# Turning five of ten groups of attention probabilities by crossbar DMA instead of on TensorE

## The chip, the cores and the metric

The kernel runs on one core of one Trainium2 chip. The metric is the device time of one launch, in microseconds. TensorE (PE) does the matrix products, VectorE (DVE), ScalarE (ACT) and GpSimd (POOL) the rest; SyncE (SP) issues nearly all transfers. All engines run side by side, each through its own instructions in order, and wait for one another by semaphores.

## What is computed

One block of a transformer on 256 rows of 1024 columns, in float32: a mixer whose first half is a pool over windows of 2, 4, 8 and 16 rows and whose second half is self-attention, then cross-attention to 256 rows of memory, then a gated feed-forward with a convolution over three rows.

```python
h = rms_norm(x, norm_mix_g); proj = h @ w_in            # u | q | k | v
q, k = rope(rms_norm(q)), rope(rms_norm(k))             # 8 heads of 64
p = softmax(causal(q @ k.T) / 8)                        # per head, 256 x 256
attn = p @ v
x = x + concat([pool(u) * pool_scale, attn]) @ w_out
h, m = rms_norm(x), rms_norm(mem)
p = softmax(rms_norm(h @ w_xq) @ rms_norm(m @ w_xk).T / 16)   # 4 heads of 256
x = x + (p @ (m @ w_xv)) @ w_xo
up = conv3(rms_norm(x) @ w_up) + conv_b                 # 2 x 2816 columns
x = x + (silu(gate) * val) @ w_down
```

The blocks of the self-attention's mixture are 256 rows long, as the sequence is, so it is plain causal attention here. A softmax is computed with its rows (queries) on partitions; the product with V needs the probabilities with their keys on partitions. So every 128x128 block of them has to be transposed, and these transposes are what the change is about.

## The kernel before

**Weights and precision.** All weights come from one packed tensor in 1 MB chunks (128x2048), loaded by SP into a ring of three buffers `raw` (L189). A chunk is two units of 128x1024. A unit is split into a high part `wh`, which ScalarE casts (L217), and a low part `wl`, the difference, from DVE (L228); a product of float32 quality is then three fast products, high by high, high by low and low by high (L421, L423, L426 in `a_chunk`, L307 and L308 in `both`). `mg` is the normed memory and `xg` the normed input, in the same two parts.

**Order.** The program order on every engine is written by hand. Side work (`score_job`, `attn_job`, `pool_job`, `key_job`, `x_job` and others) is in generators, started by `go`. The main line walks through the weight products and calls `tick()` every few products; each tick advances every live generator by one `yield`, and `wait(n)` lets n ticks pass. The tables `WAIT_SCORE`, `WAIT_ATTN`, `WAIT_POOL`, `WAIT_X` and so on hold these numbers: they decide between which weight products a step of side work is issued, on each engine it uses, its DMAs on SP among them.

**Buffers.** All products go to eight PSUM banks used as a ring, `bank()`; a new bank takes the place of an older one whose last reader has to be done. Temporaries of 128x512 come from a ring of 19, `t2`. Mean, variance and their inverse roots are small instructions; GpSimd does the longer chains (`rs4y`, `rs5y`: twelve each, L256 to L259).

**Stages.** Products k, q, v and u (unit 12 onwards is the pool's u); then, in units 18 to 25, the keys of the cross-attention from `mg`, and alongside the self-attention and the pool; then the output projection (unit 26 on, `resid_stage`), the cross queries (34), the cross values (42 to 49, with the cross-attention alongside in `x_job`), its output (50), and the feed-forward (58 on).

**Self-attention.** `scores` makes score banks for two query halves, tt = 0 and tt = 1. For tt = 1 a first product writes the causal mask into the banks (L570) and the products of q and k add to it (L579). `score_job(tt, h0, ...)` then handles one bank: row maximum (DVE, L599), `nbs` = its scaled negative (L602), exponentials with their sums (ScalarE, L608), normalisation (L610, L612), four transposes into one bank (TensorE, L618), and copies to `pt0` and `pt1` (ScalarE, L624 to L630). There are six such groups: (0,0), (0,1), (1,0), (1,1), (1,4), (1,5). `attn_job` multiplies by v (L654 to L658).

**Pool.** `pool_job` takes u from its two banks as `uh` (ScalarE) and `ul` (DVE, L284), multiplies by band matrices (L694 to L697) and scales by `rct` (DVE, `pf`, L700), then splits the outcome into `poolh` and `pooll`.

**Cross-attention.** `x_job(hp)` does heads 2hp and 2hp+1: scores, softmax into `xp` (query halves tt = 0, 1), then for each head four transposes (L902), a cast to `xpt` high (ScalarE) and its low part (DVE), and the products with `vx` (L293 to L295). So there are four groups of transposes here, and ten in all.

**Turning by DMA, as the kernel already does it elsewhere.** The normed cross keys `kn` and the last residual are turned so: an engine copies a float32 tile into two 16-bit planes (low and high halves apart; `kp`, L747), one crossbar DMA transposes 8 blocks of 128x128 16-bit values (`kf`, L755), and copies join the planes into float32 again (`kT`, L761). Every copy of the keys is ScalarE's.

## Time and profile before

| | |
|---|---|
| median of 3 runs | 377.52 us (377.51 to 377.65) |
| the profiled execution | 378.47 us, of which the span of instructions is 376.7 |
| granted TensorE clock | 1.000 of full speed |
| TensorE busy | 371.4 us of the span |
| DVE, ScalarE, GpSimd busy | 316.0, 267.2, 62.3 us |
| moved by DMA | 71.22 MB |

In the rows of the profile a line number points into the kernel before; `out<-in` gives the names without their numbers, `xN` the number of instructions in a row. In a timeline the first two columns are start and duration in microseconds, and idle time ahead of an instruction stands in brackets with what ended it. In a group the last numbers are total busy time, mean of one in ns, and idle time before it. A duration of one instruction includes its pipeline, so neighbours overlap.

### The profile page before, as it was taken

What the parts mean: (1) busy time and instruction counts of PE and PEld (TensorE: products, weight loads), DVE (VectorE), ACT (ScalarE), POOL (GpSimd) and SP (SyncE); (2) the same over time, 40 slices, a digit from 0 to 9 for tenths busy, and PEclk for the clock granted to TensorE, in tenths of its full rate; (3) what the DMA queues carried; (4) which work ended last, traced back from release to release, by engine and by line L of the source; (5) the groups of instructions that cost most, each with busy time, mean ns of one, the idle gap of its engine ahead of it and who ended that gap; (6) DMA issues with size and microseconds to landing.
All of it is one profiled execution on the core that took longest, in us unless ns stands there. A gap on an engine that the chain in (4) does not pass through costs nothing.

```text
span 376.7 us, 5788 instructions
## 1 busy us (share of the span) xinstructions
PE 371.4 (99%) x2056; PEld 319.7 (85%) x2056; DVE 316.0 (84%) x579; ACT 267.2 (71%) x507; POOL 62.3 (17%) x127
## 2 busy tenths in 40 slices
PE   8999999999999999999999999999999999999996
PEld 6888888888888988898888888888888888888885
DVE  3889999979888889979979999999999999725701
ACT  4868787987888887755664588778777787885400
POOL 0162885130861110100220000000000000000000
PEclk9999999999999999999999999999999999999999
DMA  7995481463926626442636155655555635994501
GB/s 250 420 392 179 163 329 45 187 223 121 276 54 223 224 111 225 153 182 114 213 115 231 45 195 210 223 208 169 198 209 223 224 123 213 153 322 159 204 0 56
DMA packets 20427, 71.22 MB, mean 189 GB/s; under 512 B 9776, under 2 KB 10416, under 8 KB 12848
## 3 DMA queue, kind: packets, MB, share of 16 engines
q1 hardware_dynamic: 20112, 70.34, 54.0%
q10 hardware_dynamic: 288, 0.52, 0.4%
q8 instruction: 16, 0.26, 0.3%
q14 instruction: 11, 0.09, 0.1%
HBM read 67.71 MB, written 1.05 MB: 183 GB/s over the span
## 4 chain that ended last, share of the span: by engine, by line
PE 97%; DMA 2%; SPq 0%; DVE 0%; ACT 0%; issue 0%; DVEq 0%
PE bank L308 33%; PE bank L307 17%; PE bank L421 8%; PE bank L426 8%; PE bank L423 8%; PE bank L1098 4%; PE bank L1103 4%; PE bank L1100 4%; DMA sc<-xpack 2%; PE bank L295 1%; PE bank L293 1%; PE bank L294 1%; PE bank L1120 1%; PE bank L1119 1%; PE bank L579 1%; PE bank L618 1%
## 5 line engine op out<-in xcount | busy, mean ns | idle before, releaser
L228 DVE TENSOR_TENSOR wl<-raw,wh 128x1024 fp32r<-128x1024 f32 (+1 forms) x127 | 150.4, 1196 | 10.3 <-ACT wh L217 10.1
L217 ACT CAST wh<-raw 128x1024 fp32r<-128x1024 f32 (+1 forms) x125 | 126.7, 1026 | 21.0 <-DMA raw<-wpack 20.9
L308 PE MATMUL bank<-hs,wh 128*128 128x512 f32 x304 | 105.4, 391 | 0.0
L307 PE MATMUL bank<-hs,wl 128*128 128x256 f32 x304 | 85.2, 280 | 0.0
L308 PEld LDWEIGHTS bank<-hs,wh 128*128 128x128 f32 x304 | 56.9, 187 | 12.4
L307 PEld LDWEIGHTS bank<-hs,wl 128*128 128x128 f32 x304 | 57.5, 189 | 0.0
L1017 ACT ACTIVATE y<-up,sc 128x256 f32<-128x256 f32 x44 | 26.2, 601 | 22.3 <-DVE up L1004 17.7
L308 PE MATMUL bank<-h,wh 128*128 128x512 f32 x112 | 39.4, 394 | 0.0
L1024 DVE SCALAR_TENSOR_TENSOR y<-up,sc,y 128x255 f32<-128x255 f32 (+1 forms) x88 | 36.7, 483 | 0.0
L307 PE MATMUL bank<-h,wl 128*128 128x256 f32 x112 | 31.7, 283 | 0.0
L308 PEld LDWEIGHTS bank<-h,wh 128*128 128x128 f32 x112 | 21.0, 188 | 4.7
L1098 PE MATMUL bank<-wh,act 128*128 128x512 f32 x72 | 22.2, 389 | 0.0
L1100 PE MATMUL bank<-wh,act 128*128 128x512 f32 x72 | 22.2, 389 | 0.0
L1103 PE MATMUL bank<-wl,act 128*128 128x512 f32 x72 | 22.2, 389 | 0.0
L308 PE MATMUL bank<-cat,wh 128*128 128x512 f32 x62 | 21.6, 394 | 0.0
L308 PE MATMUL bank<-ox,wh 128*128 128x512 f32 x62 | 21.6, 394 | 0.0
L421 PE MATMUL bank<-wh,xg 128*128 128x512 f32 x64 | 20.7, 405 | 0.9 <-ACT xg L278 0.8
L307 PEld LDWEIGHTS bank<-h,wl 128*128 128x128 f32 x112 | 21.1, 189 | 0.0
L421 PE MATMUL bank<-wh,mg 128*128 128x512 f32 x64 | 20.6, 403 | 0.0
L426 PE MATMUL bank<-wl,mg 128*128 128x512 f32 x64 | 20.1, 395 | 0.0
L426 PE MATMUL bank<-wl,xg 128*128 128x512 f32 x64 | 19.9, 393 | 0.0
L423 PE MATMUL bank<-wh,mg 128*128 128x512 f32 x64 | 19.9, 392 | 0.0
(263 smaller groups left out, 715.6 us busy)
## 6 DMA issues: line engine op xcount, KB each, us to landing
raw<-wpack SPq DMA_DIRECT2D x59, 1024.0 KB, 4.9
raw<-wpack SPq DMA_DIRECT2D x4, 512.0 KB, 7.8
mraw<-memT SPq DMA_DIRECT2D x4, 256.0 KB, 7.5
sc<-xpack SPq DMA_DIRECT2D x3, 256.0 KB, 6.5
raw<-wpack ACTq DMA_DIRECT2D x2, 256.0 KB, 3.6
raw<-wpack SPq DMA_DIRECT2D x2, 256.0 KB, 6.1
out<-o SPq DMA_DIRECT2D x2, 256.0 KB, 2.6
tab<-table SPq DMA_DIRECT2D x1, 480.0 KB, 8.3
```

The costliest lines, as they stand in the source:

```text
L217: copy(split[u][0][:, r], unit(u)[:, r])
L228: dve.tensor_tensor(l[:, r], unit(u)[:, r], h[:, r].bitcast(F32), op=ALU.subtract)
L307: pe.matmul(b[:, 0:n], stat[1], mov[:, 0:n], start=start, stop=False, skip_group_check=not wide_first)
L308: pe.matmul(b, stat[0], mov, start=False, stop=stop, skip_group_check=not wide_first)
L421: pe.matmul(bk[tt], a[tt][0], wv[0], start=k == 0, stop=False)
L423: pe.matmul(bk[tt], a[tt][1], wv[0], start=False, stop=False)
L426: pe.matmul(bk[tt], a[tt][0], wv[1], start=False, stop=k == KT - 1)
L1017: act.activation(y[:, g * S:(g + 1) * S], src[:, g * S:(g + 1) * S], AF.Identity, bias=col(sc, C_CB + f), scale=col(sc, C_CW + 2 * 2 * NFF ...
L1024: dve.scalar_tensor_tensor(yy[:, j:], uu[:, :S - j], col(sc, C_CW + (2 - j) * 2 * NFF + f), yy[:, j:], op0=ALU.mult, op1=ALU.add)
L1098: pe.matmul(bk[tt], a[tt][0], w[0], start=k == 0, stop=False)
L1100: pe.matmul(bk[tt], a[tt][1], w[0], start=False, stop=False)
L1103: pe.matmul(bk[tt], a[tt][0], w[1], start=False, stop=k == NFF - 1)
```

## The change

Three groups of the self-attention, (0,0), (0,1) and (1,0) (`order` 0, 1, 2), and both groups of the first two cross heads (`hp` = 0) are no longer transposed on TensorE. Their normalised probabilities are copied into 16-bit planes (`pp0`, `pp1`, `pp2`; `xpp00`, `xpp01`), transposed by a DMA from SP (`pw`, `xpf`), and joined into `pt0`, `pt1` and, for the cross heads, a new float32 tile `xT`, from which the cast and residual of `xpt` are taken. `engine(n)` picks ScalarE for 0 and GpSimd for 1: GpSimd makes all planes but `pp0`, and all joins but those of the cross half tt = 0. Of the eight joins of the cross keys (`kT`), six go from ScalarE to GpSimd. Twenty TensorE transposes and the ScalarE copies behind them go away; five DMA transposes of 256 KB come in. Beside that, numbers in the wait tables are changed, which moves other steps.

**TensorE, the scores of the second query half.** Banks 17 and 18 take the cross keys' products. Before, the mask products stand behind the pool's products with u (`misc0` and `maskr` are its bands):

```order
L694 MATMUL bank19_739<-misc0_493,uh0_676 128x256
L695 MATMUL bank19_739<-misc0_493,ul0_677 128x256
L696 MATMUL bank19_739<-maskr_77,uh1_679 128x256
L697 MATMUL bank19_739<-maskr_77,ul1_680 128x256
L421 MATMUL bank17_686<-wh19_598,mg_513 128x512
L421 MATMUL bank18_687<-wh19_598,mg_513 128x512
L423 MATMUL bank17_686<-wh19_598,mg_513 128x512
L423 MATMUL bank18_687<-wh19_598,mg_513 128x512
L570 MATMUL bank20_756<-maskr_77,identr_146 128x2x128
L570 MATMUL bank21_757<-maskr_77,identr_146 128x2x128
L570 MATMUL bank22_758<-maskr_77,identr_146 128x2x128
L570 MATMUL bank23_759<-maskr_77,identr_146 128x2x128
```

Now they stand ahead of them, among the weight products of unit 18:

```order
L431 MATMUL bank17_689<-wh18_550,mg_513 128x512
L431 MATMUL bank18_690<-wh18_550,mg_513 128x512
L433 MATMUL bank17_689<-wh18_550,mg_513 128x512
L433 MATMUL bank18_690<-wh18_550,mg_513 128x512
L580 MATMUL bank19_717<-maskr_77,identr_146 128x2x128
L580 MATMUL bank20_718<-maskr_77,identr_146 128x2x128
L580 MATMUL bank21_719<-maskr_77,identr_146 128x2x128
L580 MATMUL bank22_720<-maskr_77,identr_146 128x2x128
L589 MATMUL bank19_717<-qkT_152 128x128
L589 MATMUL bank20_718<-qkT_152 128x128
```

Between the scores of the first query half and the masks there were 40 weight products and eight pool products; now there are 28 weight products, and the pool products follow the scores. `bank21` and `bank22` take the places of the banks of u, which `uh` and `ul` read.

**DVE, on the way to the pool's second product `pf1`.** `bank27` (before) and `bank25` (now) are what `pf1` reads. Before:

```order
L599 TENSOR_REDUCE mxs_518<-bank20_756 128x2
L602 TENSOR_TENSOR nbs_519<-mxs_518,sneg_151 128x2
L599 TENSOR_REDUCE mxs_518<-bank21_757 128x2
L602 TENSOR_TENSOR nbs_519<-mxs_518,sneg_151 128x2
L228 TENSOR_TENSOR wl23_829<-raw11_546,wh23_782 128x1024
L599 TENSOR_REDUCE mxs_518<-bank22_758 128x2
L602 TENSOR_TENSOR nbs_519<-mxs_518,sneg_151 128x2
L704 TENSOR_TENSOR pooll0_750<-pf0_748,poolh0_749 128x512
L700 TENSOR_TENSOR pf1_854<-bank27_845,rct1_667 128x512
```

Now:

```order
L609 TENSOR_REDUCE mxs_518<-bank19_717 128x2
L612 TENSOR_TENSOR nbs_519<-mxs_518,sneg_151 128x2
L609 TENSOR_REDUCE mxs_518<-bank20_718 128x2
L612 TENSOR_TENSOR nbs_519<-mxs_518,sneg_151 128x2
L609 TENSOR_REDUCE mxs_518<-bank21_719 128x2
L612 TENSOR_TENSOR nbs_519<-mxs_518,sneg_151 128x2
L609 TENSOR_REDUCE mxs_518<-bank22_720 128x2
L612 TENSOR_TENSOR nbs_519<-mxs_518,sneg_151 128x2
L235 TENSOR_TENSOR wl22_796<-raw11_548,wh22_770 128x1024
L235 TENSOR_TENSOR wl23_832<-raw11_548,wh23_794 128x1024
L739 TENSOR_TENSOR pooll0_766<-pf0_764,poolh0_765 128x512
L735 TENSOR_TENSOR pf1_848<-bank25_839,rct1_665 128x512
```

All four maxima of the second query half, with their `nbs`, now precede `pf1`; three did before. Further ahead, the two `nbs` of the first half have moved from in front of `ul0` to behind `ul1`. On TensorE, unit 22 begins with `bank26` and `bank27`, and the latter takes the place of `bank25`.

**GpSimd, between the memory's norm (`vm`, `em`) and the key norm `rs4y`.** Before, nothing stands between them:

```order
L336 TENSOR_SCALAR vm_814<-vm_814 128x2
L341 TENSOR_SCALAR em_818<-vm_814 128x2
L256 TENSOR_TENSOR rs4t_969<-rs4y_968 128x4
L257 TENSOR_TENSOR rs4t_969<-rs4t_969,hm0_965 128x4
L258 TENSOR_SCALAR rs4t_969<-rs4t_969 128x4
L259 TENSOR_TENSOR rs4y_968<-rs4t_969,rs4y_968 128x4
L256 TENSOR_TENSOR rs4t_969<-rs4y_968 128x4
```

Now:

```order
L346 TENSOR_SCALAR vm_822<-vm_822 128x2
L351 TENSOR_SCALAR em_826<-vm_822 128x2
L632 COPY pp2_861<-p10_854 128x1024
L648 COPY pt0_00_711<-pw0_804 128x2x2x128
L648 COPY pt0_01_712<-pw0_804 128x2x2x128
L648 COPY pt0_10_753<-pw1_814 128x2x2x128
L648 COPY pt0_00_711<-pw2_863 128x2x2x128
L648 COPY pt1_0_860<-pw2_863 128x2x256
L263 TENSOR_TENSOR rs4t_986<-rs4y_985 128x4
L264 TENSOR_TENSOR rs4t_986<-rs4t_986,hm0_982 128x4
```

The plane of the third group and five joins come in ahead of the key norm's twelve steps; the sixth join, `pt0_11`, stands right behind those twelve. Likewise the planes `xpp00` and `xpp01` stand behind the scaling of `rs8y` (L872 before), and the DMA transposes of `xpf00` and `xpf01` on SP behind the load of chunk 27.

The diff, its tables cut to what the steps above need (line numbers in its new part are those of the changed kernel):

```diff
-WAIT_SCORE = [5, 4, 0, 9, 1, 6, 3, 1, 3, 5]
+P_POOL = [[0, 1, 1, 1, 1, 1], [1, 1, 1, 1, 1, 1]]
+P_DMA = [3]
+WAIT_SCORE = [4, 8, 0, 5, 1, 6, 3, 3, 3, 5]
...
+X_DMA = [1]
+X_POOL = [[1, 1], [0, 1, 0, 1]]
+KEY_POOL = [[0, 0, 0, 0], [1, 1, 0, 1]]
...
+    def engine(n):
+        return pool.tensor_copy if n % 2 else act.copy
 
     def col(t, c):
         return t[:, c:c + 1]
...
         dve.reciprocal(recs[:, c], sums[:, c])
         for j in range(n):
             dve.tensor_scalar(pv[:, j], pv[:, j], col(recs, tt * HEADS + h0 + 2 * j), None, op0=ALU.mult)
+        for a in range(2):
+            if (h0 % 2, a) not in pt0:
+                pt0[h0 % 2, a] = t2(f"pt0_{h0 % 2}{a}")
+        if tt and h0 < 4:
+            pt1[h0] = t2(f"pt1_{h0}")
+        order = 2 * tt + h0 % 2 + h0 // 4 * 2
+        if order < P_DMA[0]:
+            yield from wait(WAIT_P[0][order])
+            planes = t2(f"pp{order}").bitcast(U16)
+            engine(P_POOL[0][order])(
+                planes.rearrange("p (z n) -> p z n", z=2), p.bitcast(U16).rearrange("p (n z) -> p z n", z=2))
+            yield from wait(WAIT_P[1][order])
+            flat = t2(f"pw{order}").bitcast(U16)
+            nc.sync.dma_start_transpose(flat.rearrange("p (g s) -> p g s", g=8), planes)
+            yield from wait(WAIT_P[2][order])
+            for a in range(2):
+                if tt == 0:
+                    to = pt0[h0, a].bitcast(U16).rearrange("p (h q z) -> p z h q", h=2, z=2)[:, :, :, 0:P]
+                    of = flat.rearrange("p (z a h q) -> p a z h q", z=2, a=2, h=2)[:, a]
+                elif a == 0:
+                    to = pt0[h0 % 2, h0 // 4].bitcast(U16).rearrange("p (h q z) -> p z h q", h=2, z=2)[:, :, :, P:]
+                    of = flat.rearrange("p (z h k q) -> p k z h q", z=2, h=2, k=2)[:, 0]
+                else:
+                    to = pt1[h0 % 2].bitcast(U16).rearrange("p (a h q z) -> p a z h q", a=2, h=2, z=2)[:, h0 // 4]
+                    of = flat.rearrange("p (z h k q) -> p k z h q", z=2, h=2, k=2)[:, 1]
+                engine(P_POOL[1][order])(to, of)
+                yield from wait(WAIT_P[3][order])
+            return
         yield from wait(WAIT_SCORE[3])
         b = bank()
         for j in range(n):
...
         if tt == 0:
             bb = b.rearrange("p (a h q) -> p a h q", a=2, h=2)
             for a in range(2):
-                pt0[h0, a] = t2(f"pt0_{h0}{a}")
                 act.copy(pt0[h0, a].rearrange("p (h q) -> p h q", h=2)[:, :, 0:P], bb[:, a])
         else:
             bb = b.rearrange("p (h k q) -> p h k q", h=2, k=2)
             act.copy(pt0[h0 % 2, h0 // 4].rearrange("p (h q) -> p h q", h=2)[:, :, P:], bb[:, :, 0])
-            if h0 < 4:
-                pt1[h0] = t2(f"pt1_{h0}")
             act.copy(pt1[h0 % 2].rearrange("p (h q) -> p h q", h=4)[:, h0 // 4 * 2:h0 // 4 * 2 + 2], bb[:, :, 1])
         yield from wait(WAIT_SCORE[5])
 
...
                  dve.tensor_scalar(kn[c, mt][:, r], bks[mt][:, r], col(y, 2 * mt + i), None, op0=ALU.mult))
             yield from wait(WAIT_FLAT[c][mt])
             planes = t2(f"kp{c}{mt}").bitcast(U16)
-            act.copy(planes.rearrange("p (z n) -> p z n", z=2),
-                     kn[c, mt].bitcast(U16).rearrange("p (n z) -> p z n", z=2))
+            engine(KEY_POOL[0][2 * c + mt])(planes.rearrange("p (z n) -> p z n", z=2),
+                                            kn[c, mt].bitcast(U16).rearrange("p (n z) -> p z n", z=2))
             flat.append((planes, t2(f"kf{c}{mt}").bitcast(U16)))
             if mt == 0:
                 yield from wait(WAIT_KEY[2])
...
             h = 2 * c + i
             kT = t2(f"kT{c}{i}")
             for mt in range(TT):
-                act.copy(kT.bitcast(U16).rearrange("p (d m s z) -> p m z d s", d=2, m=2, z=2)[:, mt],
-                         flat[mt][1].rearrange("p (z i d s) -> p i z d s", z=2, i=2, d=2)[:, i])
+                engine(KEY_POOL[1][2 * c + i])(
+                    kT.bitcast(U16).rearrange("p (d m s z) -> p m z d s", d=2, m=2, z=2)[:, mt],
+                    flat[mt][1].rearrange("p (z i d s) -> p i z d s", z=2, i=2, d=2)[:, i])
                 yield from wait(pauses[4])
             bb = kT.rearrange("p (d s) -> p d s", d=2)
             part_h(kxv[0][:, 2 * h:2 * h + 2], bb)
...
         yield from wait(WAIT_X[4])
         if not ptv:
             ptv.extend(tiles(pair("xpt"), XH, TT, S))
+        if hp < X_DMA[0]:
+            flats = []
+            for tt in range(TT):
+                planes = t2(f"xpp{hp}{tt}").bitcast(U16)
+                engine(X_POOL[0][tt])(planes.rearrange("p (z n) -> p z n", z=2),
+                                      pvs[tt].rearrange("p h k -> p (h k)").bitcast(U16).rearrange(
+                                          "p (n z) -> p z n", z=2))
+                yield from wait(WAIT_XP[0])
+                flats.append(t2(f"xpf{hp}{tt}").bitcast(U16))
+                nc.sync.dma_start_transpose(flats[tt].rearrange("p (g s) -> p g s", g=8), planes)
+            yield from wait(WAIT_XP[1])
+            for j, h in enumerate(hs):
+                xT = t2(f"xT{hp}{j}")
+                for tt in range(TT):
+                    engine(X_POOL[1][2 * j + tt])(
+                        xT.bitcast(U16).rearrange("p (m t q z) -> p t z m q", m=2, t=2, z=2)[:, tt],
+                        flats[tt].rearrange("p (z j m q) -> p j z m q", z=2, j=2, m=2)[:, j])
+                yield from wait(WAIT_XP[2])
+                bb = xT.rearrange("p (m q) -> p m q", m=TT)
+                part_h(ptv[0][:, h], bb)
+                yield from wait(WAIT_XP[3])
+                part_l(ptv[1][:, h], bb, ptv[0][:, h])
+                yield from wait(WAIT_XP[4])
+            return
         for j, h in enumerate(hs):
             b = bank()
             bb = b.rearrange("p (m q) -> p m q", m=TT)
```

More of the change, by code (lines that the diff above doesn't have):

```diff
@@ L43 @@
 WAIT_ROPE = [6, 6, 0, 0]
-WAIT_QK = [12, 14, 11, 25, 0, 2]
-WAIT_V = [2, 10]
-WAIT_MEM = [2, 2, 5]
+WAIT_QK = [12, 14, 11, 35, 0, 2]
+WAIT_V = [2, 12]
+WAIT_MEM = [1, 2, 9]
 LATE_MEM = 6
 MEM_TICKS = 2
-WAIT_SCORE = [5, 4, 0, 9, 1, 6, 3, 1, 3, 5]
-WAIT_ATTN = [0, 15, 1, 2, 2, 0, 0]
-WAIT_POOL = [0, 8, 0, 7, 1, 5, 2, 2, 0]
+P_POOL = [[0, 1, 1, 1, 1, 1], [1, 1, 1, 1, 1, 1]]
+P_DMA = [3]
+WAIT_P = [[7, 7, 0, 0, 0, 0], [0, 0, 0, 0, 0, 0], [10, 10, 9, 6, 10, 8], [1, 7, 1, 1, 0, 1]]
+WAIT_SCORE = [4, 8, 0, 5, 1, 6, 3, 3, 3, 5]
+WAIT_ATTN = [0, 11, 1, 1, 0, 0, 0]
+WAIT_POOL = [0, 6, 0, 7, 2, 1, 3, 4, 0]
 KN_ACT = [0, 0]
@@ L55 @@
 WAIT_KEY = [1, 8, 1, 0, 0, 2, 8]
-WAIT_FLAT = [[6, 1, 2, 15, 2, 3, 2], [0, 1, 4, 38, 0, 3, 0]]
+WAIT_FLAT = [[6, 1, 2, 14, 4, 3, 2], [0, 1, 4, 39, 0, 3, 0]]
 WAIT_R1 = [5]
-WAIT_X = [3, 4, 0, 0, 8, 1, 8, 13, 8]
+X_DMA = [1]
+X_POOL = [[1, 1], [0, 1, 0, 1]]
+KEY_POOL = [[0, 0, 0, 0], [1, 1, 0, 1]]
+WAIT_XP = [1, 10, 3, 3, 2]
+WAIT_X = [3, 4, 0, 0, 8, 0, 8, 13, 8]
 WAIT_VALUE = [32]
```

## The prediction

> **What bounds the kernel now.** I read the page first, then the waits of TensorE, then the timeline of each engine around the places where the order changes. The page's line of busy time, its DVE slices and the chain by engine, then TensorE's whole list of waits:
> ```profile
> PE 371.4 (99%) x2056; PEld 319.7 (85%) x2056; DVE 316.0 (84%) x579; ACT 267.2 (71%) x507; POOL 62.3 (17%) x127
> DVE  3889999979888889979979999999999999725701
> PE 97%; DMA 2%; SPq 0%; DVE 0%; ACT 0%; issue 0%; DVEq 0%
> PE bank L421 <- ACT xg L278: 0.8, 1, 0.8
> PE bank L379 <- PEq L1232: 0.8, 1, 0.8
> ```
> TensorE is the bound and waits for nothing after its start. So every TensorE instruction removed is worth its full time, and every new TensorE wait costs its full time. The DVE row says how thin the cover is: eight or nine tenths in nearly every slice (9.4 us each), so an instruction moved ahead of something TensorE needs shows at once. The sum is made against the profiled execution, 378.47 us with a span of 376.7, which is 0.95 above the median of 377.52; I carry the difference over.
>
> **The gain: twenty transposes leave TensorE.** Groups of four, by line, and one place on the timeline (start, duration):
> ```profile
> L618 PE MATMUL bank<-tab,p 128*128 128x128 f32 x24 | 3.6, 272 | 0.0
> L902 PE MATMUL bank<-tab,xp 128*128 128x128 f32 x16 | 2.4, 272 | 0.0
> 74.22 0.61 PE L421 MATMUL bank<-wh,mg 128*128 128x512 f32 x2
> 74.67 0.62 PE L423 MATMUL bank<-wh,mg 128*128 128x512 f32 x2
> 75.13 0.60 PE L618 MATMUL bank<-tab,p 128*128 128x128 f32 x4
> 75.48 0.71 PE L426 MATMUL bank<-wl,mg 128*128 128x512 f32 x2
> 76.04 0.60 PE L618 MATMUL bank<-tab,p 128*128 128x128 f32 x4
> ```
> The mean of 272 ns is latency, since they overlap. A group holds the engine from 75.13 to 75.48, 0.35 us, and the pair of weight products behind it takes 0.56 instead of 0.45. That is 0.45 a group, and for three self-attention and two cross-attention groups 1.35 + 0.90 = 2.25 us.
>
> **First new wait, the mask products.** In the new order the four mask products of the second query half stand behind 28 weight products counted from the first scores, ahead of the pool matmuls. Two of their banks are those of the band u, which DVE must have read first.
> ```profile
> 49.14 0.73 PE L421 MATMUL bank<-wh,xg 128*128 128x512 f32 x2
> 55.62 0.61 PE L426 MATMUL bank<-wl,mg 128*128 128x512 f32 x2
> 59.32 0.63 PE L570 MATMUL bank<-maskr,identr 128*128 128x256 f32 x4
> 50.23 0.69 ACT L533 ACTIVATE v<-bank,rs2y 128x512 f32<-128x512 f32 x1
> 53.84 0.51 ACT L278 ACTIVATE mg<-mraw,sc 128x256 fp32r<-128x256 f32 x1
> 54.56 1.24 ACT L278 ACTIVATE uh<-bank,rs2y 128x512 fp32r<-128x512 f32 x2
> 54.72 0.79 DVE L602 TENSOR_TENSOR nbs<-mxs,sneg 128x4 f32<-128x4 f32 x2
> 55.42 1.40 DVE L284 SCALAR_TENSOR_TENSOR ul<-bank,rs2y,uh 128x512 fp32r<-128x512 f32 x2
> ```
> Fourteen pairs after 49.14 is 55.62; two masks (0.14 each, since the pairs' row of four lasts 0.56) bring TensorE to the first u bank at 55.9. Today that point comes at 59.32. ScalarE's cast of u now follows one piece of v in place of one piece of mg, 0.69 for 0.51, so it starts at 54.74 and its first half ends at 55.36; DVE's two residuals then end at 55.36 + 1.40 = 56.76. With one mask between, TensorE loses about 0.8 (0.5 to 1.0).
>
> **Second new wait, the first product of unit 22.** Its second bank is the one that DVE's product pf1 (L700 before) reads. Behind the u residuals DVE now has the two nbs that stood ahead of them, and a fourth maximum with its nbs, all before pf1.
> ```profile
> 59.21 1.72 DVE L612 TENSOR_SCALAR p<-p,recs 128x128 f32<-128x128 f32 x4
> 61.44 0.91 DVE L612 TENSOR_SCALAR p<-p,recs 128x128 f32<-128x128 f32 x4
> 69.51 0.68 DVE L700 TENSOR_TENSOR pf<-bank,rct 128x512 f32<-128x512 f32 x1
> 70.02 0.73 PE L421 MATMUL bank<-wh,mg 128*128 128x512 f32 x2
> 71.82 0.68 DVE L599 TENSOR_REDUCE mxs<-bank 128x2 f32<-128x512 f32 x1
> 72.54 0.16 DVE L602 TENSOR_TENSOR nbs<-mxs,sneg 128x2 f32<-128x2 f32 x1
> ```
> The residuals end at 56.76 instead of 55.42 + 1.40 = 56.82, pf1 now at 70.19; add 0.70 (nbs, 54.72 to 55.42) and 0.80 (71.82 to the next start at 72.62), take off 0.16 of idle ahead of pooll: pf1 ends near 71.5. TensorE comes to that bank at 70.02 + 0.23 - 0.90 (two groups gone) + 0.8 = 70.15. The wait is about 1.35. It falls to 0.55 if the first probabilities, now later, miss GpSimd's long accumulation (1.72 beside it, 0.91 without). After it TensorE is 0.8 + 1.35 - 0.90 = 1.25 late, and 0.8 after the third group, at attention times V. Smaller first wait, larger second: DVE's end of pf1 is the floor, so the self-attention loses rather than gains.
>
> **Third, GpSimd's queue.** Planes, joins and twelve small norm steps (first and last shown) share one in-order engine. No row shows GpSimd copying 1024 16-bit values; ScalarE's same copies and GpSimd's two-input additions are the nearest.
> ```profile
> L747 ACT COPY kp<-kn 128x1024 uint16<-128x1024 uint16 x4 | 4.2, 1050 | 1.3 <-DVE kn L744 1.2
> L761 ACT COPY kT<-kf 128x512 uint16<-128x512 uint16 x8 | 5.9, 770 | 0.0
> L353 POOL TENSOR_TENSOR accm<-sqm,accm 128x256 f32<-128x256 f32 x7 | 6.1, 878 | 0.5
> kf<-kp SPq DMA_TRANSPOSE x4, 5.0
> DMA to landing us min/median/max: 3.7/5.0/7.1
> DMA to landing us min/median/max: 3.1/7.2/8.3
> 79.85 1.14 POOL L256 TENSOR_TENSOR rs4t<-rs4y 128x4 f32<-128x4 f32 x1 [11.55 <-DVE rs4y L249]
> 83.88 0.20 POOL L259 TENSOR_TENSOR rs4y<-rs4t,rs4y 128x4 f32<-128x4 f32 x1
> 85.75 0.39 PE L654 MATMUL bank<-pt,v 128*64 128x128 f32 x4
> ```
> (The landing rows are of kf, then of the closing transposes rf, the same shape.) I take ScalarE's 1.05 a plane and 0.77 a join, the same operation and shape; 3.5 and 1.8 by the addition's rate per element is the upper end, the copy 0.5 the lower. The third plane starts behind pf1 and p10's normalisation, 72.3, ends at 73.35, lands at 78.4 by the median; two joins, 79.95. One ScalarE copy waits for this landing, with the four squares of the keys behind it (1.44); DVE's two steps bring 82.2, the norm steps 3.3 to 4.2, and the join of pt0_11, behind them on GpSimd, is ready at 86.3 to 87.2. TensorE's third bank of the product with V, which reads it, comes at 85.75 + 0.8 = 86.55. I charge 0.3 (0 to 1.4). Key joins on GpSimd I cost at nothing: TensorE needs them some 40 us after their landing; what is late if not is the sum of squares h_acc behind them.
>
> **Fourth, cross-attention.** The two planes stand on GpSimd behind the scaling of the other heads' norms, and the transposes on SP behind a 1 MB load issued at 152.31.
> ```profile
> 151.23 1.13 POOL L872 TENSOR_SCALAR rs8y<-rs8y 128x4 f32<-128x4 f32 x1 [10.94 <-DVE rs8y L254]
> 152.31 9.91 SPq L189 DMA_DIRECT2D raw<-wpack  x3
> 162.41 0.36 PE L293 MATMUL bank<-xpt,vx 128*128 128x256 f32 x1
> 163.32 0.69 DVE L282 TENSOR_TENSOR xpt<-bank,xpt 128x512 fp32r<-128x512 f32 x1 [0.26 <-ACT xpt L276]
> L276 ACT CAST xpt<-bank 128x512 fp32r<-128x512 f32 x4 | 2.3, 586 | 2.7 <-PE bank L902 2.7
> ```
> Planes end at 152.36 + 2.10 = 154.45. A landing of 5.7, between the two medians and nearer kf's, issued in pairs as here, gives 160.15. A join (0.77), the cast (0.59) and the residual (0.69) make the first head whole at about 162.2; the second needs ScalarE's own join and cast behind that, about 164.2. TensorE arrives, without its two groups, at 161.5 and at the second head's low part 1.55 later. The wait is 1.1; with 3.7 it is nothing, with 7.2 it is 2.6. Against 0.90 gained, the cross part ends 0.2 slower, between -0.9 and +1.7.
>
> **Sum.** -2.25 + 0.8 + 1.35 + 0.3 + 1.1 = +1.3: 379.8 in the profiled frame, 378.8 as a median. Its own range, with self between 0 and +1.9 and cross as above, is 376.8 to 380.3. No load limits here: the DMA row's extra 5 x 256 KB are 1.8% of 71 MB.
>
> **Rivals.**
> *Clean gain* (faster): all twenty leave and no wait comes, 377.52 - 2.25 = 375.3. For it: 0.45 a group is solid. It needs the u residuals read by 55.9 and pf1 by 70.15 in the new order; rows above put them at 56.8 and 71.5, each resting on work at both engines that is there before. Chance 0.18.
> *Half* (about the same): the cross planes land within 4.6 us, so that its wait is gone and its 0.9 is gained, 377.7; or the second wait is the short one, 0.55, 378.0. For it: kf's fastest landing was 3.7. Chance 0.22.
> *My four waits*: 378.8, chance 0.43.
> *Late landings* (slower still): rf's median of 7.2 in place of 5.0 and 5.7. The third wait grows by 2.2 to 2.5, the fourth by 1.5 to 2.6: 378.8 + 3.7 = 382.5. It decides from about 6 us. For it: rf, issued among loads as these are. Against it: kf, with a load ahead of it too, had 5.0. The Trainium skill's "VectorE: DVE Perf Modes", rules for kernel authors, speaks for this side: a 128x128 transpose belongs on TensorE if its destination may be PSUM, as here, and on the crossbar otherwise. Its table of three transpose paths gives 1309 ns a tile on the crossbar; as an estimate from that page, eight tiles in turn take 10.5 us, and the fourth wait alone would then be near 6 and the time past 383. The kf and rf rows, eight such tiles each, stay under it at 3.1 to 8.3, so the trace supports the direction and not the size. Chance 0.10.
> *GpSimd slow* (slower still): copies at twice ScalarE's time, 2.1 a plane; the cross planes end at 156.55, 2.1 later, and TensorE waits that much more, 380.9. It decides from about 1.5 a plane. Chance 0.07.
>
> **How the numbers follow.** Within 0.2% (0.76 us) is about what cannot be told from no change. Clean gain gives faster 0.18; Half gives same 0.22; the other three slower 0.60. The range takes in the clean gain and the four waits' own range, 375.2 to 380.3, and leaves out 0.17, the last two rivals.
>
> **What would show.** Right: TensorE's waits list a mask product behind DVE's ul, unit 22's first line behind pf (about 1.4), and a product with vx behind xpt; pf1 ends near 71.5; transposed planes land 5 to 7 us after issue. Wrong: no such rows, u residuals done before 55.9, or GpSimd copies far from 1.05 us. A wait at the key products or at h_acc would be one that I missed.

## The result, and the profile after

| | before | after |
|---|---|---|
| median | 377.53 us (377.51 to 377.65) | 381.81 us (381.58 to 382.17) |
| ratio | 1 | 1.0114 (95% interval 1.0096 to 1.0131) |
| the profiled execution, its span | 378.47, 376.7 | 381.92, 379.9 |

The change costs 4.28 us. The forecast was +1.3, so the side was right and the size was not: 381.81 lies 1.5 above the range. One run each of e9 and e10 below took 2106 and 1311 us and is left out, which makes their medians 380.42 and 379.99, where the expectations of e15 and e16 start from 380.68 and 380.19.

The page after, its line of busy time, the slices of DVE and GpSimd, and the chain by engine:

```profile
PE 371.4 (98%) x2036; PEld 317.2 (84%) x2036; DVE 322.7 (85%) x579; ACT 263.7 (69%) x498; POOL 83.0 (22%) x145
DVE  4789999998888989998989999999999999825701
POOL 0253887351775140330230000000000000000000
PE 63%; DVE 21%; POOL 8%; ACT 3%; issue 3%; DMA 1%; DVEq 0%; POOLq 0%
```

Twenty TensorE instructions are gone, and the chain, 97% TensorE before, now runs 29% through DVE and GpSimd. The line to stop at is DVE's: the same 579 instructions as before, and 6.7 us more of busy time (316.0 before). Apart from their order, and from two residuals of `xpt` that now read `xT` instead of a bank, these are the instructions of before; what grew is the time that they take.

TensorE's waits after, without two at the kernel's start (0.8 and 0.5):

```profile
PE bank L431 <- DVE pf L735: 1.2, 1, 1.2
PE bank L301 <- DVE xpt L289: 1.1, 1, 1.1
PE bank L301 <- DVE pooll L739: 0.5, 1, 0.5
PE bank L962 <- DVE xp L928: 0.4, 1, 0.4
PE bank L300 <- ACT xpt L283: 0.3, 1, 0.3
PE bank L580 <- DVE ul L291: 0.2, 1, 0.2
```

Three of the forecast's waits are there: the mask product behind `ul`, unit 22 behind `pf`, and the product with vx behind `xpt`. Two are new, `pooll` and `xp`. The listed numbers are smaller than what a wait costs: idle time is counted from the end of the product before, its pipeline included, and the first product behind the wait takes 0.1 to 0.2 longer to the next (0.34 instead of 0.23 in unit 22). On TensorE's timeline the four masks take from 54.85 to 55.88 instead of 0.56, the first two products of unit 22 from 68.99 to 70.88 instead of 0.46, and the two pool matmuls from 79.95 to 80.98 instead of 0.23. That is 0.47, 1.43 and 0.8 lost.

How late TensorE is at each stage, from the starts of the same instructions in both timelines (the execution after reached the first scores 0.77 earlier, at 47.28 instead of 48.05, and that is taken out):

| first instruction of | before | after | later by |
|---|---|---|---|
| attention times V (`pt`, `v`) | 84.39 | 85.66 | 2.04 |
| output projection (`cat`) | 87.16 | 88.82 | 2.43 |
| the products behind `h_acc` | 115.18 | 117.07 | 2.66 |
| attention times vx (`xpt`, `vx`) | 162.41 | 164.51 | 2.87 |
| cross output (`ox`) | 168.25 | 171.73 | 4.25 |
| feed-forward (`hs`) | 207.58 | 211.06 | 4.25 |

So the self-attention loses 2.4, the sum of squares `h_acc` 0.2 and the cross-attention 1.6. From there to the feed-forward nothing moves.

Where the self-attention loses more than forecast shows on DVE, in the stretch in which the third group is turned. The normalisations, weight splits and `pooll` after, then GpSimd's copies, then places of TensorE that follow (timeline: start, duration):

```profile
70.67 0.61 DVE L622 TENSOR_SCALAR p<-p,recs 128x256 f32<-128x256 f32 x2
71.40 1.99 DVE L622 TENSOR_SCALAR p<-p,recs 128x256 f32<-128x256 f32 x2
73.49 1.45 DVE L622 TENSOR_SCALAR p<-p,recs 128x256 f32<-128x256 f32 x2
75.05 0.62 DVE L622 TENSOR_SCALAR p<-p,recs 128x256 f32<-128x256 f32 x2
75.58 4.53 DVE L235 TENSOR_TENSOR wl<-raw,wh 128x1024 fp32r<-128x1024 f32 x3
80.03 0.68 DVE L739 TENSOR_TENSOR pooll<-pf,poolh 128x512 fp32r<-128x512 f32 x1
...
71.42 1.04 POOL L632 COPY pp<-p 128x1024 uint16<-128x1024 uint16 x1 [4.53 <-DVE recs L620]
72.39 2.40 POOL L648 COPY pt<-pw 128x512 uint16<-128x512 uint16 x3
76.51 2.58 POOL L648 COPY pt<-pw 128x512 uint16<-128x512 uint16 x2 [1.71 <-DMA pw<-pp]
86.55 0.77 POOL L648 COPY pt<-pw 128x512 uint16<-128x512 uint16 x1
...
74.65 1.52 PE L656 MATMUL bank<-tab,p 128*128 128x128 f32 x8
75.93 0.71 PE L436 MATMUL bank<-wl,mg 128*128 128x512 f32 x2
80.76 0.39 PE L301 MATMUL bank<-pooll,misc 128*128 128x256 f32 x1 [0.54 <-DVE pooll L739]
87.02 0.67 PE L689 MATMUL bank<-pt,v 128*64 128x128 f32 x3
```

The same instructions of DVE before:

```profile
71.29 0.62 DVE L612 TENSOR_SCALAR p<-p,recs 128x256 f32<-128x256 f32 x2
72.62 2.35 DVE L228 TENSOR_TENSOR wl<-raw,wh 128x1024 fp32r<-128x1024 f32 x2
75.08 0.61 DVE L612 TENSOR_SCALAR p<-p,recs 128x256 f32<-128x256 f32 x2
75.81 0.62 DVE L612 TENSOR_SCALAR p<-p,recs 128x256 f32<-128x256 f32 x2
```

A pair of normalisations takes 0.62 by itself, 1.99 beside the plane copy and a join, and 1.45 beside two joins; three weight splits take 4.53 in place of 3.5. That is 1.4 + 0.8 + 1.0 = 3.2 us more on an engine that was idle for only 0.2 in this stretch before. Two things follow on TensorE: the eight transposes at 74.65 take 1.28 to the next instruction instead of some 0.7 (two groups at 0.35) and 0.1, so that 0.5 is lost, because the last probabilities come late; and the pool matmul at 80.76 waits for `pooll`. Neither was in the forecast. The last join, at 86.55, is the forecast's third wait: the products at 87.02 that read it lose 0.39.

The tiles `pw`, `xpf`, `xp` and `kf`: GpSimd's copies of each kind (minimum, median and maximum in ns, first and last start), and from issue to landing for the first two:

```profile
L648 POOL COPY pt<-pw x6: 766/867/1747, 72.4 to 86.5; 128x512 uint16<-128x512 uint16 x6
DMA to landing us min/median/max: 4.0/7.5/8.1
...
L947 POOL COPY xT<-xpf x2: 1394/1560/1725, 162.4 to 163.7; 128x512 uint16<-128x512 uint16 x2
DMA to landing us min/median/max: 4.8/5.0/5.2
...
L937 POOL COPY xpp<-xp x2: 1037/1040/1042, 155.1 to 156.1; 128x1024 uint16<-128x1024 uint16 x2
...
L796 POOL COPY kT<-kf x6: 772/1218/1744, 108.8 to 138.1; 128x512 uint16<-128x512 uint16 x6
```

Alone, GpSimd copies a plane in 1.04 and a join in 0.77, which is what the forecast took. Beside DVE a join takes 0.85 to 1.75, and the plane of the second group takes 2.08, beside a split that keeps its 1.22 (DVE, then GpSimd):

```profile
62.49 1.22 DVE L235 TENSOR_TENSOR wl<-raw,wh 128x1024 fp32r<-128x1024 f32 x1
...
62.53 2.08 POOL L632 COPY pp<-p 128x1024 uint16<-128x1024 uint16 x1
```

So either of the two engines can be the one that is held up. TensorE does not wait for that plane. The two landings of 7.5 and 8.1 belong to the first two groups, whose joins come only at 72.4; the third, on which TensorE depends, took 4.0.

The cross-attention's end after, on the timelines of GpSimd, ScalarE, DVE and TensorE:

```profile
162.41 3.03 POOL L947 COPY xT<-xpf 128x512 uint16<-128x512 uint16 x2 [5.25 <-PE bank L962]
...
163.84 0.62 ACT L283 CAST xpt<-xT 128x512 fp32r<-128x512 f32 x1 [0.64 <-POOL xT L947]
...
164.75 1.18 DVE L289 TENSOR_TENSOR xpt<-xT,xpt 128x512 fp32r<-128x512 f32 x1
...
165.99 0.38 PE L301 MATMUL bank<-xpt,vx 128*128 128x256 f32 x1 [1.09 <-DVE xpt L289]
```

The second plane was landed at about 162.4 (issued at 157.5). Two joins of 1.5 instead of 0.77 stand beside DVE's splits, and the residual of the first head takes 1.18 instead of 0.69 beside the second join.

### The profile page after: what moved, and what is told of

It is laid out like the page before. It is cut to its first block, busy times and chain, and to the rows that moved or that the text cites. A ratio compares the mean times of both kernels' runs of the same rounds, so it can differ in the third digit from the quotient of the medians.

```text
span 379.9 us, 5768 instructions
## 1 busy us (share of the span) xinstructions
PE 371.4 (98%) x2036; PEld 317.2 (84%) x2036; DVE 322.7 (85%) x579; ACT 263.7 (69%) x498; POOL 83.0 (22%) x145
## 4 chain that ended last, share of the span: by engine, by line
PE 63%; DVE 21%; POOL 8%; ACT 3%; issue 3%; DMA 1%; DVEq 0%; POOLq 0%
PE bank L315 25%; PE bank L314 13%; DVE wl L235 8%; PE bank L1163 4%; PE bank L1158 4%; PE bank L1160 4%; PE bank L431 2%; PE bank L436 2%; PE bank L433 2%; POOL accm L363 2%; DVE p L622 1%; DVE sc L844 1%; ACT wh L224 1%; DVE kx L289 1%; PE bank L1180 1%
## 5 line engine op out<-in xcount | busy, mean ns | idle before, releaser
L431 PE MATMUL bank<-wh,mg 128*128 128x512 f32 x64 | 20.4, 398 | 1.2 <-DVE pf L735 1.2
L431 PE MATMUL bank<-wh,xg 128*128 128x512 f32 x64 | 20.4, 399 | 0.5 <-DVE wh L224 0.5
L433 PE MATMUL bank<-wh,xg 128*128 128x512 f32 x64 | 19.9, 392 | 0.0
```

The costliest lines, as they stand in the source:

```text
L431: pe.matmul(bk[tt], a[tt][0], wv[0], start=k == 0, stop=False)
L433: pe.matmul(bk[tt], a[tt][1], wv[0], start=False, stop=False)
```

## The experiments

Two theories. *Contention*: GpSimd's copies slow the DVE instructions beside them, and DVE is the engine on which TensorE waits. *Order*: the new tables put DVE's work too late, and GpSimd is only a bystander. A third suspect is late landings. Every kernel ran beside the kernel before on the same chip; that one's median was 377.40 to 377.56.

**e1: copies that nobody reads, in the kernel before.**

```diff
+        if (tt, h0) == (1, 0):
+            idle_copies(p)     # GpSimd: one plane of p, five joins within a spare tile
```

> The kernel before, with six GpSimd copies added that nothing reads: one plane copy of the first normalised probabilities of the second query half and five copies of 512 16-bit values behind it, in the stretch from about 71 to 79 us. TensorE, DVE and ScalarE keep their instructions and order. Contention theory: copies and DVE's work on tiles in the scratch memory hold each other up; the normalisations of the next groups (0.62 a pair before) and the low parts wl (1.18 each) there become 1.5 to 2 times as long while a copy runs, DVE's busy time rises by 2 to 3 us from 316.0, copies of 512 take 0.8 to 1.5; the time rises by 0 to 0.8, since TensorE has slack there (377.5 to 378.3). Order theory and late-landing theory: DVE's durations stay at 0.62 and 1.18, busy time 316, 377.5.

378.15 us, ratio 1.0013 (1.0003 to 1.0022). Its timelines of DVE and GpSimd:

```profile
70.38 1.77 DVE L620 TENSOR_SCALAR p<-p,recs 128x256 f32<-128x256 f32 x2
72.08 0.67 DVE L607 TENSOR_REDUCE mxs<-bank 128x2 f32<-128x512 f32 x1
75.85 1.50 DVE L620 TENSOR_SCALAR p<-p,recs 128x256 f32<-128x256 f32 x2
...
71.22 5.98 POOL L597 COPY spare<-spare 128x512 uint16<-128x512 uint16 x5
```

With no new order and no transfer, the pairs go from 0.62 to 1.77 and 1.50, and each copy takes 1.2. The maximum, whose input is a PSUM bank, keeps its 0.67. Contention is real; here most of it falls into slack, so it costs 0.7 by the medians (0.1 to 0.8 by the interval).

**e2: the self-attention's planes and joins on ScalarE.**

```diff
-P_POOL = [[0, 1, 1, 1, 1, 1], [1, 1, 1, 1, 1, 1]]
+P_POOL = [[0, 0, 0, 0, 0, 0], [0, 0, 0, 0, 0, 0]]
```

> The changed kernel, with the one GpSimd-made planes and six joins of the self-attention on ScalarE instead; TensorE, DVE and SP keep their order. Contention theory: the normalisations at 71 to 75 us go from 1.99 and 1.45 back to 0.62 a pair, the three wl behind from 4.53 to 3.5, and TensorE's waits for the last probabilities (0.5), for the pool's low part (0.7) and inside the product with V (0.4) go: 381.8 - 1.6 = 380.2; ScalarE's 7 us of copies may take back up to 1. Order theory: the loss lies in the masks and in unit 22's wait alone, 381.8. Late landings: unchanged or worse, 381.8.

386.25, ratio 1.0223 (1.0199 to 1.0247): far off. The normalisations are back at 0.62 a pair, but ScalarE has a queue of its own; its timeline:

```profile
70.78 1.05 ACT L632 COPY pp<-p 128x1024 uint16<-128x1024 uint16 x1 [2.85 <-DVE p L622]
```

The plane waits 2.85 for its probabilities, with six exponentials behind it, and those are late for everything that follows: TensorE waits 2.1 for `cat`. The run shows DVE undisturbed, and does not price the contention.

**e3: the cross planes and joins on ScalarE.**

```diff
-X_POOL = [[1, 1], [0, 1, 0, 1]]
+X_POOL = [[0, 0], [0, 0, 0, 0]]
```

> The changed kernel, with both planes and all four joins of the cross heads on ScalarE instead of GpSimd; TensorE, DVE and SP keep their order. Contention theory: GpSimd's joins took 1.39 and 1.73 against ScalarE's 0.77, and DVE's residual beside them 1.18 against 0.68; on ScalarE the first head is whole about 1 us earlier and the cross-attention loses 0.6 instead of 1.6: 380.8, if the planes go out no later. Late landings: the wait follows the landing, 5 us behind the plane, and stays: 381.8.

382.43, ratio 1.0137 (1.0117 to 1.0156): a miss too. The wait for the low part of `xpt` falls from 1.1 to 0.7, and that for the high part rises from 0.3 to 1.1. The transposes are issued 1.1 earlier (155.15 instead of 156.21) but land in 6.0 to 6.4 instead of 4.8 to 5.2, and ScalarE's joins wait for them; why they land later stays open. So the run does not price the cross copies on GpSimd.

**e4: the six changed tables of before, the same groups on DMA.**

```diff
-WAIT_QK = [12, 14, 11, 35, 0, 2]
-WAIT_SCORE = [4, 8, 0, 5, 1, 6, 3, 3, 3, 5]
+WAIT_QK = [12, 14, 11, 25, 0, 2]
+WAIT_SCORE = [5, 4, 0, 9, 1, 6, 3, 1, 3, 5]
...
```

(WAIT_V, WAIT_MEM, WAIT_ATTN and WAIT_POOL too are those of the kernel before.)

> The changed kernel with the six wait tables of the scores, pool, memory, values and norms as in the kernel before, so that the masks stand behind the pool products again and only three maxima ahead of pf1; the same groups go by DMA. Order theory: the waits at the masks (0.47 in all) and at unit 22 (1.44) go, 381.8 - 1.9 = 379.9. Contention theory: these waits go too, but GpSimd's copies now meet the normalisations at another place, and part comes back: 379.9 to 381. Late landings: the planes come no earlier, 381.8 or more.

381.13, ratio 1.0097 (1.0082 to 1.0112), 0.1 above the range given for contention. Of TensorE's waits:

```profile
PE bank L689 <- POOL pt L648: 1.3, 1, 1.3
PE bank L431 <- DVE pf L735: 1.1, 1, 1.1
```

The mask's wait is gone with the order. The wait at `pf` stays: when TensorE comes 0.9 earlier, it meets DVE there, in either order. At the start of attention times V this kernel stands where before stands (0.1 ahead), three groups lighter; then the last join is late by 1.3, at GpSimd. The order alone is not what loses the time.

**e5: the cross groups back on TensorE.**

```diff
-X_DMA = [1]
-WAIT_X = [3, 4, 0, 0, 8, 0, 8, 13, 8]
+X_DMA = [0]
+WAIT_X = [3, 4, 0, 0, 8, 1, 8, 13, 8]
```

> The changed kernel with the cross heads' two groups back on TensorE, as in the kernel before; self-attention and key joins as changed. All theories put the cross part at what the two traces differ by there, 1.6: 381.8 - 1.6 = 380.2. Contention theory adds that GpSimd's key joins still hold up DVE (kx residuals 1.2 instead of 0.69).

380.27, ratio 1.0076 (1.0052 to 1.0100). The cross part costs 381.81 - 380.27 = 1.54.

**e6 and e7: the self groups back on TensorE, and everything back, under the new tables.**

```diff
-P_DMA = [3]
+P_DMA = [0]
...
+X_DMA = [0]                                  # e7 only
+KEY_POOL = [[0, 0, 0, 0], [0, 0, 0, 0]]      # e7 only
```

> The changed kernel with the three self-attention groups back on TensorE but its own wait tables kept; cross heads and key joins as changed. Order theory: masks and maxima stand where they cost 1.9, and the gain of 1.35 is gone too, so the time rises or stays: 381.8 to 383. Contention theory: the nine copies' hold on DVE at 62 to 79 us goes, pf1 comes 0.4 earlier, and the late last probabilities and pool part (1.2) and the late join (0.4) go: 377.5 + 0.8 (order) + 0.2 + 1.6 = 380.1.

> The changed kernel's wait tables with every group on TensorE and every key join on ScalarE: the order alone. Order theory: 377.5 + 1.9 = 379.4. Contention theory: pf1 ends only 0.7 later than in the kernel before, and the wait at the masks is taken up in that: 378.2 to 378.5.

388.94 and 388.39, ratios 1.0299 (1.0274 to 1.0323) and 1.0294 (1.0254 to 1.0334). Both are misses. A group on TensorE uses up other ticks than one on DMA, so every later step shifts, and the cross keys end late (TensorE waits 4.4 and 5.8 for `kx`). Up to there e7 says something: at the output projection it is 1.25 behind before, with a wait at `pf` of 0.2. With the gain of 1.35 in hand the wait at `pf` is 1.2. So 0.9 of the gain, the two groups that leave ahead of `pf`, becomes waiting there.

**e8: the key joins on ScalarE.**

```diff
-KEY_POOL = [[0, 0, 0, 0], [1, 1, 0, 1]]
+KEY_POOL = [[0, 0, 0, 0], [0, 0, 0, 0]]
```

> The changed kernel with the six key joins back on ScalarE; TensorE and DVE keep their order. Contention theory: the wait at h_acc (0.22) goes and DVE's kx residuals fall from 1.2 to 0.69, so that the norms of the next heads, 0.84 late, come earlier and the cross planes with them: 381.8 - 0.2 - 0.5 = 381.1, unless ScalarE becomes late there. Order and late-landing theories: 381.6 to 381.8.

381.55, ratio 1.0104 (1.0081 to 1.0127): by the time alone not told from 381.81. In the trace the step at `h_acc` is gone.

**e9: the self-attention's six joins on ScalarE, planes as they are.**

```diff
-P_POOL = [[0, 1, 1, 1, 1, 1], [1, 1, 1, 1, 1, 1]]
+P_POOL = [[0, 1, 1, 1, 1, 1], [0, 0, 0, 0, 0, 0]]
```

> The changed kernel with the planes as they are and only the six joins of the self-attention moved from GpSimd to ScalarE; TensorE, DVE and SP keep their order. It parts what the second run lost: there the third plane stood on ScalarE ahead of the exponentials. Contention theory: the second pair of normalisations is held up by the plane alone (about 1.0 to 1.2 in place of 1.99), the third falls to 0.62 and the three wl to 3.5; TensorE's waits for the last probabilities and the pool part (1.2) go, and the join behind the norm steps (0.4). Against that ScalarE has 4.6 more ahead of and among the key squares: 380.2 if its slack holds, up to 383 if the norm steps and cat come late. Order theory: 381.8 plus what ScalarE loses.

380.42, ratio 1.0078 (1.0064 to 1.0093), 1.4 faster than after. In this stretch only the pair beside the plane is still slow; the waits at the last probabilities and at `pooll` are gone, and one of 0.6 at `cat` is new. DVE, then GpSimd:

```profile
70.68 1.47 DVE L622 TENSOR_SCALAR p<-p,recs 128x256 f32<-128x256 f32 x2
72.26 0.61 DVE L622 TENSOR_SCALAR p<-p,recs 128x256 f32<-128x256 f32 x2
...
70.71 1.04 POOL L632 COPY pp<-p 128x1024 uint16<-128x1024 uint16 x1 [4.52 <-DVE recs L620]
```

**e10: the third group back on TensorE.**

```diff
-P_DMA = [3]
+P_DMA = [2]
```

> The changed kernel with two self-attention groups by DMA instead of three: the third, whose plane and two joins lie right beside DVE's normalisations, is back on TensorE (+0.45). Contention theory: three of eight copies leave the stretch of 71 to 79 us, DVE there is 1.5 shorter, TensorE's 1.2 of waits shrink to 0.3: 381.8 + 0.45 - 0.9 = 381.3. Order theory: 381.8 + 0.45 = 382.3.

379.99, ratio 1.0068 (1.0051 to 1.0086): 1.8 faster with 0.45 more work on TensorE, and 1.3 below the time given for contention. So the third group on DMA costs about 2.3 us to save 0.45. Three joins of the first two groups still stand beside DVE's normalisations and slow them:

```profile
71.60 1.63 DVE L622 TENSOR_SCALAR p<-p,recs 128x256 f32<-128x256 f32 x2
```

But the three splits behind are back at 3.48, and TensorE waits neither for the last probabilities nor for `pooll`.

**e11 and e12: the old order, two early groups on DMA, cross and keys back; in e12 also `pooll` of the first half moved behind `pf` of the second.** The edits of e4, e5 and e8, WAIT_FLAT as before, and

```diff
-P_POOL = [[0, 1, 1, 1, 1, 1], [1, 1, 1, 1, 1, 1]]
+P_POOL = [[1, 1, 1, 1, 1, 1], [1, 1, 1, 1, 1, 1]]
-P_DMA = [3]
-WAIT_P = [..., [1, 7, 1, 1, 0, 1]]
+P_DMA = [2]
+WAIT_P = [..., [0, 0, 1, 1, 0, 1]]
...
             dve.tensor_tensor(pf, b, rct[g2], op=ALU.mult)
+            for args in late:                    # e12 only
+                dve.tensor_tensor(*args, op=ALU.subtract)
```

> The order of the kernel before, cross heads and key joins as there, and only the first two groups (ready 10 us earlier) by DMA, planes and four joins on GpSimd, the last join ahead of the norm steps. TensorE loses 0.9 of work. What I now think: unit 22's first products wait for pf1, whose end DVE sets, so 0.9 earlier on TensorE is 0.9 of wait: 377.5 to 378.2, with a wait of 0.8 to 1.1 behind pf in the list. If the wait there came from the moved maxima and nbs (order theory), it is absent in this order: 376.7.

> As the run before it, with one DVE instruction moved: the low part of the pool's first half (0.61) behind pf1 instead of ahead of it. DVE as the floor: pf1 ends 0.6 earlier, the wait behind pf falls from about 1.0 to 0.4 and the time by as much, below the kernel before: 376.9 to 377.4. Order theory: no change against the run before it.

379.63 and 380.14, ratios 1.0051 (1.0036 to 1.0066) and 1.0067 (1.0055 to 1.0078): 1.4 and 2.7 above their ranges. Neither gains. In both, GpSimd makes two planes beside DVE's splits ahead of `pf`. In e11 the first of these splits:

```profile
61.49 2.06 DVE L235 TENSOR_TENSOR wl<-raw,wh 128x1024 fp32r<-128x1024 f32 x1
```

It takes 2.06 and the next 1.45 instead of 1.21, `pf` ends 1.0 later behind the first scores than in the kernel before, and the wait there is 1.8 instead of 0.8 to 1.1. Further on ScalarE's exponentials stop for a landing that the expectation had not counted (ScalarE, then DVE):

```profile
71.78 0.56 ACT L618 ACTIVATE p<-bank,nbs,sp 128x256 f32<-128x256 f32 x1 [3.75 <-DMA pw<-pp]
...
73.02 0.17 DVE L620 RECIPROCAL recs<-sums 128x2 f32<-128x2 f32 x1 [1.97 <-ACT p L618]
```

What they write is a new tile `p`, from the ring of 19; that its place was still held by planes under transfer is how I read the row, and no run tests it. In e12 the wait at `pf` falls from 1.8 to 1.2, and that at `poolh` rises from 0.4 to 1.0: in neither of these two orders are both early.

**e13: no copies at all.** The run that decides: the planes and joins of the three self groups are left out, and what is left stands where it stood.

```diff
-            engine(P_POOL[0][order])(planes..., p...)
-            nc.sync.dma_start_transpose(flat..., planes)
+            nc.sync.dma_start_transpose(flat..., p.bitcast(U16))
...
-                engine(P_POOL[1][order])(to, of)      # V's products read flat instead
```

> The changed kernel without the planes and joins of its three self-attention groups: the DMA turns the normalised tile as it lies, and the products with V read the landed tile directly (their numbers are then meaningless; the normalisation adds a constant so that they stay finite). Every instruction that is left stands where it stood. If GpSimd's copies cost TensorE its time by slowing VectorE beside them, the waits at the last probabilities (0.5), at pooll (0.7) and behind the last join (0.39) all go: 381.8 - 1.6 = 380.2, between 379.9 and 380.6, the wait at pf stays above 0.8, and VectorE's pairs of normalisations take 0.62 each. If VectorE is late by its order alone, only the join's wait goes: 381.4. If what the crossbar transposes themselves do costs something, it stays too: 381.4 or above.

379.66, ratio 1.0057 (1.0042 to 1.0072). DVE's timeline in the same stretch, and TensorE's wait at `pf`:

```profile
71.47 0.62 DVE L627 TENSOR_SCALAR p<-p,recs 128x256 f32<-128x256 f32 x2
72.19 0.62 DVE L627 TENSOR_SCALAR p<-p,recs 128x256 f32<-128x256 f32 x2
73.45 3.48 DVE L235 TENSOR_TENSOR wl<-raw,wh 128x1024 fp32r<-128x1024 f32 x3
```

```profile
PE bank L431 <- DVE pf L728: 1.1, 1, 1.1
```

2.15 us come back, 0.24 more than the range given for contention; in the profiled executions 1.8, all of it ahead of the output projection, where TensorE is 0.65 late (2.43 after). The transfers are still there, landing in 4.9 to 7.8, so they are not what cost the time. The order is still there too, and DVE's normalisations and splits in it take their old time again. The run takes out all nine copies, one plane of ScalarE's among them, and with them the late join; so 2.15 is what the copies cost together.

**e14, e15, e16: the cross groups and key joins back, beside e13, e9 and a form of e10 whose joins are on ScalarE.**

```diff
+X_DMA = [0]                                  # all three, with WAIT_X of before
+KEY_POOL = [[0, 0, 0, 0], [0, 0, 0, 0]]      # all three
...
+P_POOL = [[0, 1, 1, 1, 1, 1], [0, 0, 0, 0, 0, 0]]    # e15 and e16
+P_DMA = [2]                                  # e16
```

> The same, and the two cross groups back on TensorE with the key joins on ScalarE. The contention theory: 380.2 less 1.54 (cross) and 0.26 (keys), 378.4, between 378.1 and 378.9: what is left above 377.5 is the mask wait and the pf wait less three groups, 0.47 + 1.44 - 1.35 = 0.6. The order theory: 381.4 - 1.8 = 379.6.

> Planes as in the changed kernel, self joins on ScalarE, cross groups back on TensorE, key joins on ScalarE. If the three costs add up: 380.68 - 1.54 - 0.26 = 378.9, between 378.5 and 379.4. If the cross part had only been hiding behind the self-attention's delay, above 379.4.

> Two groups of the self-attention on DMA with their joins on ScalarE, the rest back. By adding up: 380.19 - 1.54 - 0.26 = 378.4, less up to 0.4 for joins that leave GpSimd: 378.0 to 378.5. A version that gains over the kernel before would be below 377.1; the wait at pf (1.2 in the changed kernel) is the reason why none of the theories puts it there.

378.11, 379.02 and 378.59, ratios 1.0020 (1.0011 to 1.0030), 1.0046 (1.0030 to 1.0062) and 1.0031 (1.0018 to 1.0044). The first two lie in their ranges, e16 is 0.1 above. Against e13, e9 and e10 they are 1.55, 1.40 and 1.40 lower (key joins included; e16 has its self joins on ScalarE besides): the cross part's cost adds to the self part's, whatever the self part does. No version came below the kernel before. In this order the floor is e14: even with copies that cost nothing, two waits on DVE outweigh three groups by 0.7.

So the loss has three parts, each from a run. By medians: what e14 has left, 0.71; the cross groups with the key joins, 1.55 (e13 to e14); the copies in the self-attention, eight of nine GpSimd's, 2.15 (after to e13); 4.4 with 4.28 measured. By the trace: 0.65, then 1.60 + 0.22 at `h_acc`, then 1.78; 4.25 of 4.25.

## Why the prediction was wrong, step by step

- *The gain, 2.25*: right, as far as runs show it. In e13 and e14 two waits of 0.47 and 1.43 against three groups at 0.45 make +0.55; 0.65 and 0.71 were measured.
- *First wait*, forecast 0.8 (0.5 to 1.0): 0.47. The `ul` residuals ended 0.5 earlier than forecast, at 55.50 (56.27 with the offset of 0.77). ScalarE's cast ahead of `uh`, which waits for a weight chunk, had started 0.84 earlier than before (51.28 and the offset, against 52.89).
- *Second wait*, forecast 1.35: 1.43, and `pf` ended at 71.26 with the offset, forecast 71.5. The reason given, DVE's `pf` as a floor, held in every run with DMA groups; e4 shows that it does so in the old order too. The first two waits together were 1.90 for a forecast of 2.15, so the loss beyond the forecast lies elsewhere.
- *Third, GpSimd's queue*, forecast 0.3: 0.39, by the join of `pt0_11` behind the norm steps as described.
- *The failed step* is in that same third part: "Planes, joins and twelve small norm steps share one in-order engine". GpSimd was priced as a queue, and a copy by its own duration, which was right (1.04 and 0.77 alone). What a copy does to DVE beside it was given no term. It was 3.2 us of DVE's time between 71.4 and 80.1. On TensorE it cost 0.5 at the last probabilities and 0.8 at `pooll`, which with the late join is 1.7 of the 1.8 that e13 takes off. The page of before had the hint: normalisations of 1.72 beside GpSimd's long accumulation and 0.91 without were quoted in the second wait, and used only to shorten it.
- *Key joins on GpSimd at nothing*: 0.22 at `h_acc`, the place named as late if not. Small, and gone in e8.
- *Fourth, cross-attention*, forecast 1.1 gross: about 2.5 gross, 1.6 net (1.54 by e5). The landing was 5.0 instead of 5.7. The joins took 1.4 and 1.7 instead of 0.77, the residual 1.18 instead of 0.69: the same missing term, as the trace reads; e5 gives its size and no run its cause, since e3 met later landings. Beside it `xp` of the other heads came 0.4 late, and GpSimd's planes began 0.8 later against TensorE than forecast, because the sums `ssx` did; with the key joins on ScalarE (e8) they still did, and why stays open.
- *Late landings* had nearly this time, 382.5, by another mechanism. Landings of 7.5 and 8.1 came, but where nobody waited. So the nearness of that rival's number is luck. *GpSimd slow* had the wrong form: by itself the engine was as fast as ScalarE, and beside DVE one of the two paid, GpSimd too in the plane of 2.08 and the cross joins.
- *The range*: its own bounds, self to +1.9 and cross to +1.7, add up to 381.1 and not to 380.3; the measured 381.81 lies above either.

The Trainium skill has the missing term. "SBUF — State Buffer", who interferes with whom, says that VectorE and GpSimd share a pair of ports as an exclusive lock, which whoever comes first holds for a whole instruction; VectorE instructions with two inputs in SBUF contend with GpSimd's reads, as do those in a two-port mode, which `tensor_scalar` can enter. The longest normalisation agrees in size:

```profile
L622 DVE TENSOR_SCALAR p<-p,recs x16: 273/408/1204, 58.8 to 75.3; 128x128 f32<-128x128 f32 x8, 128x256 f32<-128x256 f32 x8
```

The one of 1.20 started at 71.40, beside the plane copy that ran from 71.42 to 72.46, and ended at 72.60: nearly its own 0.35 and the whole copy. By these starts, 0.02 apart, DVE came first and still paid, so the trace does not show that the order decides. The two-input splits agree in kind, at 1.5 each instead of 1.18, less than a full copy each, and so does the plane of 2.08, which started behind its split. That the maximum kept its 0.67 agrees with the same section's exemption of instructions with at most one input in SBUF outside such a mode.

## What to carry to other kernels

Work taken off the bound engine is worth only what the next engine allows: here DVE ended `pf` only 0.06 us before TensorE needed it (70.19 and 70.25 before), and 0.9 of 1.35 us gained turned into waiting there. When the moved work lands on GpSimd, price it twice, once as its own duration and once as the delay of the normalisations and two-input splits that DVE runs beside it, and put it where DVE has slack (the third group's turn by DMA cost about 2.3 us; in e11 the first two groups' planes alone moved `pf` by 1.0). A cheap test comes first: added copies that nobody reads, in the unchanged kernel.

## What was not expected of the hardware

A 0.35 us DVE instruction took 1.20 beside one GpSimd copy, while the copy kept its 1.04; at 62.5 it was the copy that took 2.08, while DVE's split kept its 1.22. Six copies cost 0.7 us in the kernel before (e1); the nine of the changed kernel, six of them in the same stretch, cost about 1.8 (after against e13, at the output projection). Landings of crossbar transposes of one size spread from 3.1 to 8.5 us in the kernel after.
